# A hybrid mLSTM and attention layer: the first block's squares on two engines, its norm in two GpSimd operations, its rounded copy ahead of the weights' low parts

## The chip, the cores and the metric

The kernel runs on one core of a Trainium2 chip. The metric is the device time of one execution in microseconds (us). Before the change the median of three runs was 689.77 us (689.24 to 689.87).

The engines are called by their names or by the profile's short ones: TensorE (PE for matmuls, PEld for its weight loads), VectorE (DVE), ScalarE (ACT), GpSimd (POOL), SyncE (SP, which here only issues DMAs). Each engine has its own stream of instructions and works it off in order. Engines wait for each other by semaphores.

## The reference

The layer takes x (512 tokens by 1024 channels, float32). What the change touches is its start: the RMS norm of the rows and the first columns of one large projection.

```python
def rmsnorm(x, w):
    y = x * lax.rsqrt(jnp.mean(x * x, axis=-1, keepdims=True) + EPS)
    return y * w

h = rmsnorm(x, norm_w)
proj = jnp.einsum('bsd,de->bse', h, w_in) + b_in      # 1024 -> 11272 columns
# split of proj: mLSTM q, k, v, gates; attention q, k, v; output gates; merge gates
qs = rmsnorm(to_heads(sq, 8), sb_q_norm_w)
# ... mLSTM in chunks, stick-breaking attention, two projections, gated merge
out = x + jnp.einsum('bsd,de->bse', merged, w_out)
```

## The kernel before

All matmuls are made from float32 numbers split in a high part (rounded to the format that TensorE takes at full rate) and a low part (the rest). A product is three matmuls: high by high, low by high and high by low. For the activations the parts are called hh and hl, for the weights wh and wl, and for the weights of the first group fh and fl.

The work is a list of units in a fixed order, one slab of weights (512 KB) each. Each unit has a load (SP), a split (ScalarE writes the high part, VectorE the low part), 24 matmuls, and an evacuation from PSUM. Attention heads and mLSTM heads are interleaved with the units by a table of start numbers. Nothing in this order is decided at run time: every engine gets its instructions in the order in which the code emits them.

The first four units are special. They hold the weights of attention's q (512 columns of 1024 rows, in four slabs of 256 rows), and each of the four token blocks (tb, 128 tokens) passes through all of them, as soon as its own norm is done. For one block:

- `x_norm` (line 281): the sum of squares of each row. For block 0, whose x arrives in two halves, ScalarE squares one half after the other (line 289), and GpSimd adds the two sums (line 290). `rstd` (line 273) then turns the sum into r = (sum/1024 + eps)^-0.5 with two GpSimd operations.
- `x_mul` (line 296): VectorE multiplies x by r in place.
- `x_tp` (line 301): TensorE transposes x, eight times 128 by 128, into two PSUM tiles of four each.
- `x_hh` (line 307): VectorE reads one PSUM tile, multiplies by the norm's weights nw_t and writes hh, rounded. `x_hl` (line 313) writes hl = the same product minus hh, in four instructions per PSUM tile.
- `first_hi` (line 1158) writes the high parts fh of the weights on ScalarE, `first_lo` (line 1164) the low parts fl: for k = 2 and 3 on GpSimd, for the others on VectorE. k numbers the eight groups of 128 channels.
- `first_mm` (line 1208) emits the matmuls of one block: for block 0 those of k = 0 to 4, then the transposes of block 1, and then k = 5 to 7.

Ahead of all that, TensorE runs nine matmuls on zeros (`warm(9)`, line 1186). Then come `norm_vec` (line 229), which turns the norm's weights by a TensorE transpose and copies them to nw_t on VectorE, `x_scale(0)` (`x_norm` and `x_mul` of block 0) and two more matmuls on zeros. The order of the emission is:

```python
warm(9)
norm_vec()
x_scale(0)
warm(2)
first_hi(0); first_lo(0); first_lo(1)
x_turn(0)        # x_tp, x_hh, x_hl of each of the two PSUM tiles
first_hi(1); first_lo(2, nc.gpsimd); first_lo(3, nc.gpsimd)
x_norm(1); first_hi(2); first_lo(4); x_mul(1); first_lo(5)
```

Of the kernel before, what the change touches and what calls it, by code (L numbers as in the profile page):

```python
# [11 lines left out]
AF = mybir.ActivationFunctionType  # L12
OP = mybir.AluOpType

D = 1024
T = 512
KT = 8
TB = 4
NQK = 18
EPS = 1e-6  # L20
# [15 lines left out]
def tile_hybrid_layer(  # L36
# [16 lines left out]
    nc = tc.nc  # L53
# [21 lines left out]
    def blk(tag, dt=F32, shape=(512,), name=None, p=128):  # L75

        where = mp if tag in MISC else sp
        return where.tile([p] + list(shape), dt, name=name or tag, tag=tag, bufs=BUFS[tag])

    def two(tag, dt=F32, name=None):  # L80

        t = blk(tag, dt, (2, 512), name=name)
        return t[:, 0, :], t[:, 1, :]

    def dense_ps():
        return psd.tile([128, 512], F32, name="dps", tag="dps")

    def att_ps():
        return psa.tile([128, 512], F32, name="aps", tag="aps")
# [100 lines left out]
    def h_sta(k, tb):  # L190
        ts = slice(tb * 128, (tb + 1) * 128)
        return hh[:, k, ts], hl[:, k, ts]
# [27 lines left out]
    mhalf = cst.tile([128, 8], F32, name="mhalf")  # L220
# [6 lines left out]
    nw_t = cst.tile([128, 8], F32, name="nw_t")  # L227

    def norm_vec():
        vp = att_ps()  # L230
        nc.tensor.transpose(vp[:, 0:8], v_rows[0:8, :], ident[0:8, 0:8])
        nc.vector.tensor_copy(nw_t, vp[:, 0:8])

    def load_vecs():
        for j in range(4):
# [37 lines left out]
    def rstd(dst, ssq, n, eps):  # L273
        nc.gpsimd.tensor_scalar(dst, ssq, 1.0 / n, eps, op0=OP.mult, op1=OP.add)
        nc.gpsimd.tensor_tensor(dst, dst, mhalf[:, 0:dst.shape[1]], op=OP.pow)

    def x_scale(tb):
        x_norm(tb)
        x_mul(tb)

    def x_norm(tb):
        xs = tiny.tile([128, 4], F32, name="xs", bufs=2)
        ssq, r = xs[:, 0:2], xs[:, 2:3]
        xn = x_t[tb]
        junk = blk("om", BF, (D,), name="junk")
        if tb == 0:
            for i in range(2):
                c = slice(i * D // 2, (i + 1) * D // 2)
                nc.scalar.activation(junk[:, c], xn[:, c], AF.Square, accum_out=ssq[:, i:i + 1])
            nc.gpsimd.tensor_tensor(ssq[:, 0:1], ssq[:, 0:1], ssq[:, 1:2], op=OP.add)  # L290
        else:
            nc.scalar.activation(junk, xn, AF.Square, accum_out=ssq[:, 0:1])
        rstd(r, ssq[:, 0:1], D, EPS)
        x_r.append(r)

    def x_mul(tb):
# [4 lines left out]
    def x_tp(tb, g):  # L301
        tp = x_ps[tb, g] = att_ps()
        for j in range(4):
            kt = g * 4 + j
            nc.tensor.transpose(tp[:, j * 128:(j + 1) * 128], x_t[tb][:, kt * 128:(kt + 1) * 128], ident)  # L305

    def x_hh(tb, g):
        ks = slice(4 * g, 4 * g + 4)
        nc.vector.tensor_tensor(hh[:, ks, tb * 128:(tb + 1) * 128],
                                x_ps[tb, g].rearrange("p (k t) -> p k t", k=4),  # L310
                                nw_t[:, ks].unsqueeze(2).to_broadcast([128, 4, 128]), op=OP.mult)

    def x_hl(tb, *ks):
        ts = slice(tb * 128, (tb + 1) * 128)
        for k in ks:
            tp = x_ps[tb, k // 4][:, k % 4 * 128:k % 4 * 128 + 128]
            nc.vector.scalar_tensor_tensor(hl[:, k, ts], tp, nw_t[:, k:k + 1],  # L317
                                           hh[:, k, ts].bitcast(F32), op0=OP.mult, op1=OP.subtract)

    def x_turn(tb):  # L320
        for g in range(2):
            x_tp(tb, g)
            x_hh(tb, g)
            x_hl(tb, *range(4 * g, 4 * g + 4))
# [831 lines left out]
    f_w = []  # L1156

    def first_hi(i):
        his = two("qk", FR, name="fh")
        for j in range(2):  # L1160
            nc.scalar.activation(his[j], units[i].st[:, j, :], AF.Copy)
            f_w.append((his[j], blk("y", FR, name="fl")))

    def first_lo(k, engine=nc.vector):
        hi, lo = f_w[k]
        engine.tensor_tensor(lo, units[k // 2].st[:, k % 2, :], hi.bitcast(F32), op=OP.subtract)
# [15 lines left out]
    def warm(n):  # L1182
        for _ in range(n):
            nc.tensor.matmul(wp, idle[:, 0:128], idle, start=True, stop=True)

    warm(9)
    norm_vec()
    x_scale(0)
    warm(2)
    first_hi(0)  # L1190
    first_lo(0)
    first_lo(1)
    x_turn(0)
    first_hi(1)
    first_lo(2, nc.gpsimd)
    first_lo(3, nc.gpsimd)
    x_norm(1)
    first_hi(2)
    first_lo(4)
# [5 lines left out]

    f_ps = []

    def first_mm(tb):
        def mm(half):
            if half == 0:  # L1210
                f_ps.append(dense_ps())
            n = 4 if tb else 5
            for k in range(n) if half == 0 else range(n, KT):
                sh, sl = h_sta(k, tb)
                wh, wl = f_w[k]
                nc.tensor.matmul(f_ps[tb], sh, wh, start=k == 0, stop=False)  # L1216
                nc.tensor.matmul(f_ps[tb], sl, wh, start=False, stop=False)  # L1217
                nc.tensor.matmul(f_ps[tb], sh, wl, start=False, stop=k == KT - 1)  # L1218
        return mm

    for tb in range(TB):
        units[tb].mm = first_mm(tb)
# [40 lines left out]
    for c in range(N):  # L1263
# [15 lines left out]
        if c == 0:  # L1279
            x_tp(1, 0)  # L1280
            x_tp(1, 1)
            x_hh(1, 0)
            x_hl(1, 0, 1, 2, 3)
            x_norm(2)
            x_mul(2)
            x_hh(1, 1)
            x_hl(1, 4, 5, 6, 7)
            x_scale(3)
            gates_fill()
# [47 lines left out]
```

## Time and profile before

| | |
|---|---|
| median of the runs | 689.77 us |
| the profiled execution, its own time | 689.49 us |
| its span, first to last instruction | 687.8 us |
| TensorE matmuls busy | 681.0 us (99%) |
| VectorE | 467.2 us (68%) |
| ScalarE | 337.1 us (49%) |
| GpSimd | 111.7 us (16%) |

1.7 us of the execution's time lie outside the span. Times in rows count from the start of the span. A matmul's busy time is modelled and overlaps with the next one's, so the distance from one start to the next tells more than the duration. A row that merges several instructions has the time from the start of the first to the end of the last.

### The profile page before, as it was taken

The page shows a single profiled execution, that of the slowest core. Times are in us where ns is not written, and L with a number is a line of the kernel's source. Part 1 is how long each engine was busy: PE and PEld are TensorE (multiplying, and loading weights), DVE is VectorE, ACT ScalarE, POOL GpSimd, SP SyncE. Part 2 cuts the span into 40 slices and gives each one's busy share as a digit, 9 for nine tenths or more (in the row PEclk, how much of TensorE's full clock was granted, in tenths as well). Part 3 has the DMA queues.
Part 4 walks back from the last instruction along what each step waited for, and adds up shares of the span by engine and source line. Part 5 has one row for each costly group of instructions (what it writes and reads, how often), then busy time and mean ns, then how long its engine had stood idle before and what let it go on. Part 6 is the DMA issues. An engine that isn't in the chain of part 4 may idle for free.

```text
span 687.8 us, 9389 instructions
## 1 busy us (share of the span) xinstructions
PE 681.0 (99%) x3162; PEld 568.9 (83%) x3162; DVE 467.2 (68%) x819; ACT 337.1 (49%) x631; POOL 111.7 (16%) x266
## 2 busy tenths in 40 slices
PE   8999999999999999999999999999999999999997
PEld 5888888888888888888888888888888888888876
DVE  6746787777997886789834648994352364445997
ACT  6245465566455653344466533448554343344451
POOL 4122042365430310000001210000112000111020
PEclk9999999999999999999999999999999999999999
DMA  7433543435463533643341343434223456599333
GB/s 250 139 95 107 160 138 105 134 112 149 134 171 86 124 111 83 139 95 92 107 117 53 107 109 85 128 91 134 68 64 90 115 176 200 141 206 205 121 82 103
DMA packets 122289, 84.74 MB, mean 123 GB/s; under 512 B 19018, under 2 KB 105956, under 8 KB 122240
## 3 DMA queue, kind: packets, MB, share of 16 engines
q1 hardware_dynamic: 119600, 77.97, 40.3%
q0 software_dynamic: 2496, 6.03, 4.7%
q8 instruction: 25, 0.41, 0.2%
q14 instruction: 24, 0.20, 0.1%
q10 hardware_dynamic: 144, 0.13, 0.1%
HBM read 66.22 MB, written 2.15 MB: 99 GB/s over the span
## 4 chain that ended last, share of the span: by engine, by line
PE 98%; DVE 1%; DMA 1%; SPq 0%; issue 0%; ACT 0%
PE dps L92 28%; PE dps L93 27%; PE dps L94 27%; PE aps L93 3%; PE aps L94 3%; PE aps L92 3%; PE dps L1216 1%; PE dps L1217 1%; PE dps L1218 1%; PE aps L811 1%; PE aps L813 1%; PE aps L812 1%; DMA stg<-in_w_in_dram 1%; PE aps L305 0%; DVE hl L317 0%; PE aps L591 0%
## 5 line engine op out<-in xcount | busy, mean ns | idle before, releaser
L98 DVE TENSOR_TENSOR wl<-stg,wh 128x1024 fp32r<-128x1024 f32 x92 | 112.5, 1223 | 106.0 <-ACT wh L97 105.5
L92 PE MATMUL dps<-hh,wh 128*128 128x512 f32 x448 | 175.0, 391 | 0.0
L94 PE MATMUL dps<-hh,wl 128*128 128x512 f32 x448 | 174.4, 389 | 0.0
L93 PE MATMUL dps<-hl,wh 128*128 128x512 f32 x448 | 174.4, 389 | 0.0
L97 ACT ACTIVATE wh<-stg 128x1024 fp32r<-128x1024 f32 x92 | 96.8, 1052 | 64.5 <-PE dps L94 44.3
L94 PEld LDWEIGHTS dps<-hh,wl 128*128 128x128 f32 x448 | 84.1, 188 | 17.7
L93 PEld LDWEIGHTS dps<-hl,wh 128*128 128x128 f32 x448 | 84.2, 188 | 16.8
L92 PEld LDWEIGHTS dps<-hh,wh 128*128 128x128 f32 x448 | 84.1, 188 | 16.7
L92 PE MATMUL dps<-wh,hh 128*128 128x512 f32 x224 | 87.7, 392 | 0.0
L94 PE MATMUL dps<-wh,hl 128*128 128x512 f32 x224 | 87.3, 390 | 0.0
L93 PE MATMUL dps<-wl,hh 128*128 128x512 f32 x224 | 87.2, 389 | 0.0
L94 PEld LDWEIGHTS dps<-wh,hl 128*128 128x128 f32 x224 | 42.0, 188 | 9.0
L92 PEld LDWEIGHTS dps<-wh,hh 128*128 128x128 f32 x224 | 42.1, 188 | 8.3
L93 PEld LDWEIGHTS dps<-wl,hh 128*128 128x128 f32 x224 | 42.1, 188 | 8.2
L704 DVE SCALAR_TENSOR_TENSOR acc<-tmp,vec,acc 128x511 f32<-128x511 f32 (+2 forms) x48 | 36.0, 750 | 1.7
L707 ACT ACTIVATE tmp<-acc 128x512 f32<-128x512 f32 x16 | 10.1, 633 | 50.8 <-DVE acc L704 50.8
L480 POOL TENSOR_SCALAR_AFFINE_SELECT om<-om 128x128 f32<-128x128 f32 x32 | 15.3, 479 | 96.2 <-ACT om L478 96.1
L486 DVE TENSOR_TENSOR_SCAN om<-om 128x512 f32<-128x512 f32 (+3 forms) x32 | 26.7, 834 | 5.5 <-POOL om L480 5.5
L764 POOL TENSOR_SCALAR_AFFINE_SELECT w_all<-om 128x128 f32<-128x128 f32 x16 | 5.3, 363 | 144.4 <-DMA om<-rb_d 144.4
L478 ACT ACTIVATE om<-aps,rq 128x512 f32<-128x512 f32 (+3 forms) x32 | 16.8, 524 | 21.0 <-PE aps L94 21.0
L94 PE MATMUL dps<-yh,wl 128*128 128x512 f32 x64 | 24.9, 389 | 0.0
L92 PE MATMUL dps<-yh,wh 128*128 128x512 f32 x64 | 24.9, 389 | 0.0
(249 smaller groups left out, 1217.8 us busy)
## 6 DMA issues: line engine op xcount, KB each, us to landing
stg<-in_w_in_dram SPq DMA_DIRECT2D x87, 512.0 KB, 3.9
az<-ay SPq DMA_DIRECT2D x128, 40.0 KB, 2.9
stg<-in_w_proj_s_dram SPq DMA_DIRECT2D x8, 512.0 KB, 4.7
B<-in_w_out_dram SPq DMA_DIRECT2D x8, 512.0 KB, 6.6
stg<-in_w_proj_m_dram SPq DMA_DIRECT2D x8, 512.0 KB, 5.9
wl<-stg POOLq DMA_DIRECT2D x8, 512.0 KB, 5.9
tz<-ty SPq DMA_DIRECT2D x72, 32.0 KB, 1.9
brow<-in_b_in_dram SPq DMA_DIRECT2D x8, 256.0 KB, 4.5
```

The costliest lines, as they stand in the source:

```text
L92: nc.tensor.matmul(ps, ah, bh, start=first, stop=False)
L93: nc.tensor.matmul(ps, ah, bl, start=False, stop=False)
L94: nc.tensor.matmul(ps, al, bh, start=False, stop=last)
L97: nc.scalar.activation(hi, src, AF.Copy)
L98: nc.vector.tensor_tensor(lo, src, hi.bitcast(F32), op=OP.subtract)
L478: nc.scalar.activation(om[:, 0:n], zp, AF.Sigmoid, scale=rn[:, h:h + 1])
L480: nc.gpsimd.affine_select(out=om[:, ts], in_=om[:, ts], compare_op=OP.is_gt, fill=1.0, base=0, channel_multiplier=1, pattern=[[-1, 128]])
L486: nc.vector.tensor_tensor_scan(back, back, back, 1.0, op0=OP.mult, op1=OP.bypass)
L704: nc.vector.scalar_tensor_tensor(acc[:, j:], t[:, 0:T - j], cw(3 - j, ch), acc[:, j:], op0=OP.mult, op1=OP.add)
L707: nc.scalar.activation(t, acc, AF.Sigmoid)
L811: nc.tensor.matmul(nm[:, 0:258], ph, vh, start=j == 0, stop=False)
L812: nc.tensor.matmul(sum_v, ph, vl, start=False, stop=False)
```

## The change

Four things change, all in the first block's path.

1. The sum of squares of block 0: ScalarE squares only the first half; VectorE squares the second half, with a scalar_tensor_tensor that also accumulates.
2. The norm: GpSimd no longer adds the two sums in an operation of its own. One tensor_scalar adds both sums and 1024·eps, and the power follows. The factor 32 (the root of 1024) that this leaves out is put into nw_t, whose copy becomes a multiplication. The other blocks have the same form with two operations, as before.
3. On VectorE, hh of the first PSUM tile now stands ahead of fl of k = 0 and 1. On TensorE both transposed tiles are emitted first, as they were executed before.
4. TensorE's first six matmuls of block 0 are reordered: high by high of k = 0 and 1, then the two with fl, then the two with hl.

```diff
     def norm_vec():
         vp = att_ps()
         nc.tensor.transpose(vp[:, 0:8], v_rows[0:8, :], ident[0:8, 0:8])
-        nc.vector.tensor_copy(nw_t, vp[:, 0:8])
+        nc.vector.tensor_scalar(nw_t, vp[:, 0:8], 32.0, None, op0=OP.mult)
...
         if tb == 0:
-            for i in range(2):
-                c = slice(i * D // 2, (i + 1) * D // 2)
-                nc.scalar.activation(junk[:, c], xn[:, c], AF.Square, accum_out=ssq[:, i:i + 1])
-            nc.gpsimd.tensor_tensor(ssq[:, 0:1], ssq[:, 0:1], ssq[:, 1:2], op=OP.add)
+            a, b = xn[:, 0:D // 2], xn[:, D // 2:D]
+            nc.scalar.activation(junk[:, 0:D // 2], a, AF.Square, accum_out=ssq[:, 0:1])
+            nc.vector.scalar_tensor_tensor(junk[:, D // 2:D], b, 1.0, b, op0=OP.mult, op1=OP.mult,
+                                           accum_out=ssq[:, 1:2])
+            nc.gpsimd.tensor_scalar(r, ssq[:, 0:1], ssq[:, 1:2], D * EPS, op0=OP.add, op1=OP.add)
         else:
             nc.scalar.activation(junk, xn, AF.Square, accum_out=ssq[:, 0:1])
-        rstd(r, ssq[:, 0:1], D, EPS)
+            nc.gpsimd.tensor_scalar(r, ssq[:, 0:1], 1.0, D * EPS, op0=OP.mult, op1=OP.add)
+
+        nc.gpsimd.tensor_tensor(r, r, mhalf[:, 0:1], op=OP.pow)
         x_r.append(r)
...
     first_hi(0)
+    x_tp(0, 0)
+    x_tp(0, 1)
+    x_hh(0, 0)
     first_lo(0)
     first_lo(1)
-    x_turn(0)
+    x_hl(0, 0, 1, 2, 3)
+    x_hh(0, 1)
+    x_hl(0, 4, 5, 6, 7)
     first_hi(1)
...
+    def three(tb, k, *which):
+        sh, sl = h_sta(k, tb)
+        wh, wl = f_w[k]
+        for n in which:
+            nc.tensor.matmul(f_ps[tb], *((sh, wh), (sl, wh), (sh, wl))[n],
+                             start=(k, n) == (0, 0), stop=(k, n) == (KT - 1, 2))
...
             for k in range(n) if half == 0 else range(n, KT):
-                sh, sl = h_sta(k, tb)
-                wh, wl = f_w[k]
-                nc.tensor.matmul(f_ps[tb], sh, wh, start=k == 0, stop=False)
-                nc.tensor.matmul(f_ps[tb], sl, wh, start=False, stop=False)
-                nc.tensor.matmul(f_ps[tb], sh, wl, start=False, stop=k == KT - 1)
+
+                if tb or k > 1:
+                    three(tb, k, 0, 1, 2)
+                elif k == 0:
+                    three(tb, 0, 0)
+                    three(tb, 1, 0)
+                    three(tb, 0, 2)
+                    three(tb, 1, 2)
+                    three(tb, 0, 1)
+                    three(tb, 1, 1)
         return mm
```

The start of VectorE's stream before, with what each instruction waits for in brackets (a semaphore of an engine, or of a DMA queue, DMAHW; x is the block's x, xs the small tile with the sums and r):

```order
L1179 MEMSET idle 128x512
L232 COPY nw_t<-aps 128x8 [waits PE_49]
L297 TENSOR_SCALAR x<-x,xs 128x1024 [waits DMAHW0_49,DMAHW1_49,Activation_49,Pool_49]
L1166 TENSOR_TENSOR fl<-stg,fh 128x512 [waits DMAHW3_49,Activation_49]
L1166 TENSOR_TENSOR fl<-stg,fh 128x512 [waits Activation_49]
L309 TENSOR_TENSOR hh<-aps,nw_t 128x4x128 [waits DVE_49,PE_49]
L317 SCALAR_TENSOR_TENSOR hl<-aps,nw_t,hh 128x128 [waits DVE_49]
```

and the same place now:

```order
L1182 MEMSET idle 128x512
L232 TENSOR_SCALAR nw_t<-aps 128x8 [waits PE_49]
L289 SCALAR_TENSOR_TENSOR junk,xs<-x 128x512 [waits DMAHW1_49]
L300 TENSOR_SCALAR x<-x,xs 128x1024 [waits DVE_49,DMAHW0_49,Activation_49,Pool_49]
L312 TENSOR_TENSOR hh<-aps,nw_t 128x4x128 [waits PE_49]
L1169 TENSOR_TENSOR fl<-stg,fh 128x512 [waits DMAHW3_49,Activation_49]
L1169 TENSOR_TENSOR fl<-stg,fh 128x512 [waits Activation_49]
L320 SCALAR_TENSOR_TENSOR hl<-aps,nw_t,hh 128x128 [waits DVE_49]
```

The square (line 289) has come in between nw_t, which waits for TensorE, and the multiplication of x; hh stands ahead of the two fl.

TensorE's stream from the first group of zeros to the first matmuls of block 0, before:

```order
L1184 MATMUL dps<-idle 128x512 x9
L231 MATMUL aps<-ident,v_rows 128x8
L1184 MATMUL dps<-idle 128x512 x2
L305 MATMUL aps<-ident,x 128x128 x8
L1216 MATMUL dps<-fh,hh 128x512
L1217 MATMUL dps<-fh,hl 128x512
L1218 MATMUL dps<-fl,hh 128x512
L1216 MATMUL dps<-fh,hh 128x512
```

and now:

```order
L1187 MATMUL dps<-idle 128x512 x9
L231 MATMUL aps<-ident,v_rows 128x8
L1187 MATMUL dps<-idle 128x512 x2
L308 MATMUL aps<-ident,x 128x128 x8
L1220 MATMUL dps<-fh,hh 128x512 x2
L1220 MATMUL dps<-fl,hh 128x512 x2
L1220 MATMUL dps<-fh,hl 128x512 x2
L1220 MATMUL dps<-fh,hh 128x512
```

The transpose of the norm's weights (line 231) stays behind the nine matmuls on zeros; of the first six matmuls only the order is another.

## Rows read from the trace of the kernel before

**Rows 1.** What TensorE waited for, in the whole span: engine, line, who released it; us in total, times, longest.

```profile
PE dps L1184 <- DVE idle L1179: 1.5, 1, 1.5
PE dps L1216 <- DVE hh L309: 1.0, 1, 1.0
PE aps L305 <- DVE x L297: 0.8, 2, 0.6
```

**Rows 2.** Busy time in three stretches: from and to, length; then busy us (and instructions) of PE, PEld, DVE, ACT, POOL; clock, DMA share, GB/s.

```profile
9.20:13.20 4.00, 3.92 (x15) 2.69 (x15) 3.96 (x12) 3.49 (x7) 2.90 (x4) 1.00 1.06 405
...
14.20:653.00 638.80, 638.80 (x2975) 535.45 (x2974) 429.22 (x758) 313.97 (x597) 103.16 (x247) 1.00 0.45 121
...
657.50:684.00 26.50, 26.50 (x130) 22.39 (x128) 24.68 (x36) 9.39 (x12) 1.77 (x2) 1.00 0.33 90
```

**Rows 3.** Two pieces of the chain that ended last, in order of time: start, us, what.

```profile
6.48 0.64 ACT fh L1161
...
12.47 0.76 DVE x L297
```

**Rows 4.** VectorE's timeline of the first 18 us: start, us, instruction, count, idle time before it and its releaser.

```profile
5.81 0.17 DVE L232 COPY nw_t<-aps 128x8 f32<-128x8 f32 x1 [4.36 <-PE aps L231]
6.26 0.75 DVE L297 TENSOR_SCALAR x<-x,xs 128x1024 f32<-128x1024 f32 x1 [0.28 <-POOL xs L275]
7.14 1.29 DVE L1166 TENSOR_TENSOR fl<-stg,fh 128x512 fp32r<-128x512 f32 x2
8.35 0.68 DVE L309 TENSOR_TENSOR hh<-aps,nw_t 128x512 fp32r<-128x512 f32 x1
9.07 1.13 DVE L317 SCALAR_TENSOR_TENSOR hl<-aps,nw_t,hh 128x128 fp32r<-128x128 f32 x4
...
12.47 0.74 DVE L297 TENSOR_SCALAR x<-x,xs 128x1024 f32<-128x1024 f32 x1
13.14 0.68 DVE L1166 TENSOR_TENSOR fl<-stg,fh 128x512 fp32r<-128x512 f32 x1
13.74 1.28 DVE L1166 TENSOR_TENSOR fl<-P,fh 128x512 fp32r<-128x512 f32 x2
...
16.70 1.37 DVE L297 TENSOR_SCALAR x<-x,xs 128x1024 f32<-128x1024 f32 x1
```

**Rows 5.** ScalarE's timeline at the start, the same columns.

```profile
3.55 0.63 ACT L289 ACTIVATE junk<-x 128x512 bf16<-128x512 f32 x1 [1.49 <-DMA x<-in_x_dram]
...
4.30 0.63 ACT L289 ACTIVATE junk<-x 128x512 bf16<-128x512 f32 x1
4.84 0.19 ACT L289 ACTIVATION_READ_ACCUMULATOR junk<-x 128x1 f32 x1
```

**Rows 6.** GpSimd's timeline of the first 18 us.

```profile
5.11 0.19 POOL L290 TENSOR_TENSOR xs<-xs 128x1 f32<-128x1 f32 x1 [3.67 <-ACT junk L289]
5.39 0.19 POOL L274 TENSOR_SCALAR xs<-xs 128x1 f32<-128x1 f32 x1
5.66 0.56 POOL L275 TENSOR_TENSOR xs<-xs,mhalf 128x1 f32<-128x1 f32 x1
8.79 2.56 POOL L1166 TENSOR_TENSOR fl<-stg,fh 128x512 fp32r<-128x512 f32 x2 [2.57 <-ACT fh L1161]
11.43 0.19 POOL L274 TENSOR_SCALAR xs<-xs 128x1 f32<-128x1 f32 x1
...
14.46 0.62 POOL L274 TENSOR_SCALAR xs<-xs 128x1 f32<-128x1 f32 x1 [2.19 <-ACT junk L292]
...
16.56 0.96 POOL L572 MEMSET wg<- 128x1024 f32 x1
```

**Rows 7.** TensorE's timeline up to the first matmul of block 0.

```profile
1.50 4.11 PE L1184 MATMUL dps<-idle 128*128 128x512 f32 x9 [1.50 <-DVE idle L1179]
5.55 0.22 PE L231 MATMUL aps<-ident,v_rows 8*128 8x8 f32 x1
5.70 0.73 PE L1184 MATMUL dps<-idle 128*128 128x512 f32 x2
7.07 1.09 PE L305 MATMUL aps<-ident,x 128*128 128x128 f32 x8 [0.63 <-DVE x L297]
9.18 0.47 PE L1216 MATMUL dps<-fh,hh 128*128 128x512 f32 x1 [1.02 <-DVE hh L309]
```

**Rows 8.** Groups of instructions on VectorE by line, operation and shape: count, busy us, mean ns of one, idle us before them and its releaser.

```profile
L710 DVE SCALAR_TENSOR_TENSOR tmp<-acc,tmp 128x512 f32<-128x512 f32 x16 | 11.0, 688 | 2.7 <-ACT tmp L707 2.7
L486 DVE TENSOR_TENSOR_SCAN om<-om 128x512 f32<-128x512 f32 x8 | 9.8, 1227 | 5.1 <-POOL om L480 5.1
...
L487 DVE TENSOR_TENSOR a_all<-a_all,om 128x256 f32<-128x256 f32 x8 | 3.6, 452 | 0.8
```

**Rows 9.** GpSimd's timeline at 94.3 us, one row.

```profile
94.26 0.29 POOL L483 TENSOR_SCALAR_AFFINE_SELECT a_all<-a_all 128x128 f32<-128x128 f32 x1
```

**Rows 10.** VectorE's timeline at the same moment.

```profile
94.32 0.51 DVE L487 TENSOR_TENSOR a_all<-a_all,om 128x256 f32<-128x256 f32 x1
```

**Rows 11.** GpSimd's timeline at 137 us.

```profile
137.14 0.82 POOL L378 TENSOR_SCALAR rq<-rq 128x4 f32<-128x4 f32 x1
```

**Rows 12.** VectorE's timeline at the same moment.

```profile
136.64 1.22 DVE L98 TENSOR_TENSOR wl<-stg,wh 128x1024 fp32r<-128x1024 f32 x1 [2.67 <-ACT wh L97]
137.78 0.68 DVE L98 TENSOR_TENSOR qtt<-tz,qtt 128x512 fp32r<-128x512 f32 x1
```

## The prediction

> **What bounds the kernel now.** First the list of what TensorE waited for. It has three entries in the whole span: 1.5 us for the zeros, 1.0 us for the first hh and 0.8 us for the scaled x, all in the first 14 us [rows 1]. Next the busy time by stretches: from 14.20 us on TensorE is busy for every microsecond, 638.80 of 638.80 and 26.50 of 26.50 [rows 2]. So whatever moves the end of the start-up moves the end of the kernel by as much, and no later wait takes it up. Third the chain of waits: it runs through ScalarE's fh at 6.48 us and then through VectorE up to the multiplication of block 1's x at 12.47 us, to which TensorE's transposes of block 1 are tied [rows 3]. That multiplication is the gate. TensorE can do the matmuls of block 0 early or late, but behind k = 4 it needs block 1's x. Last the timelines of the engines, for how VectorE gets from 7.14 us, where its dense work begins, to that gate at 12.47 us: 5.33 us without a pause of note [rows 4].
>
> **What the change moves, step by step.**
>
> *The square on VectorE.* Before, ScalarE squared the halves at 3.55 and 4.30 us, the second accumulator was read by 5.03 us [rows 5], and GpSimd added (5.11), scaled (5.39) and took the power (5.66 to 6.22) [rows 6]. VectorE multiplied x at 6.26 us [rows 4]. Now VectorE's half of the square is emitted behind nw_t, and nw_t waits for TensorE's transpose of the norm's weights, which stands behind the nine matmuls on zeros and ran at 5.55 to 5.77 us [rows 7]. nw_t ran at 5.81 to 5.98 us after 4.36 us of idling [rows 4]. VectorE works in order, so the square can't start before about 5.95 us, although its half of x was there by 4.30 us, when ScalarE began on it without a wait [rows 5]. Queued behind it are x's multiplication and all that follows; GpSimd's sum waits for it, and TensorE for both.
>
> The trace has no such square. Its nearest rows are the scalar_tensor_tensor of the same size, 0.69 us, and as an upper end the scan of that size, 1.23 us [rows 8]. I take 0.69, the same operation, and 0.10 for reading the accumulator, which on ScalarE ended that much behind the ACTIVATE (4.93 against 5.03 [rows 5]). Below zero it can't be. The sum is there at 5.95 + 0.69 + 0.10 = 6.74 us.
>
> *The norm in two operations.* GpSimd starts 0.08 us later (as 5.03 to 5.11), the power 0.27 us after that (5.39 to 5.66) and takes 0.56 us, and VectorE follows 0.04 us behind [rows 4, 6]: 6.82, 7.09, 7.65, and x's multiplication at 7.69 us. That is 1.43 us later than before. The removed addition is worth 0.28 us (5.11 to 5.39 [rows 6]) and is contained in this. The factor 32 in nw_t costs nothing: one instruction on 8 columns for another; half or double its 0.17 us would move the sum by no more than 0.2.
>
> *hh ahead of fl.* x's multiplication takes 0.75 us, to 8.44. TensorE begins 0.06 us later (7.01 to 7.07 [rows 4, 7]) at 8.50. Eight transposes took 1.09 us, so the first four are out after about 0.62, and hh starts near 9.16 us. Before, the two fl filled just this wait (7.14 to 8.35 [rows 4]); now VectorE idles there and does them afterwards. Its sum up to the gate stays nearly as it was: hl behind hh cost 0.72 us from start to start because it needs hh, and an unrelated instruction 0.60 (13.14 to 13.74) [rows 4], so 5.33 becomes 5.21. Without any collision the gate would be at 9.16 + 5.21 = 14.37 us, 1.90 later. The matmuls' new order gains nothing, because TensorE waits at the gate anyway.
>
> *The collision.* Before, VectorE's two fl were over at 8.43 us, and GpSimd's two fl ran from 8.79 to 11.35 us beside hh and hl, which read PSUM [rows 4, 6]. GpSimd's start hangs on ScalarE and the weights and stays. VectorE's fl now come at 9.76 us, in the middle of them, and all four read two operands from SBUF. The trace shows that such pairs don't run side by side. VectorE's multiplication at 16.70 us took 1.37 us instead of 0.74 while a GpSimd memset ran from 16.56 [rows 4, 6]. GpSimd's 0.19 us operation took 0.62 at 14.46 us, when VectorE was in an fl [rows 4, 6]. A VectorE tensor_tensor that began 0.06 us into a GpSimd select took 0.51 us, with a mean of 0.452 for its form [rows 8 to 10], as if it had started 0.17 us before the select's end. And a GpSimd operation that came in during a VectorE subtraction ended 0.10 us behind it, although the next VectorE subtraction was already queued [rows 11, 12]: whoever waits gets in between two instructions.
>
> So I have them take turns. GpSimd's first fl holds until 8.79 + 1.28 - 0.17 = 9.90; VectorE's first goes from 9.90 to 10.58; GpSimd's second, due at 10.07, gets in at about 10.50 and holds until 10.50 + 1.28 - 0.17 = 11.61; VectorE's second starts there, and hl 0.60 later at 12.21 us, against 9.07 before [rows 4]. That is 3.14 us, and from hl to the gate nothing differs. The second block's r is ready well before the gate: GpSimd's two operations on it follow on its second fl with 0.83 us between them (5.39 to 6.22 [rows 6]).
>
> The Trainium skill, "SBUF — State Buffer", section "Who interferes with whom", states the rule in the same sense: a VectorE instruction with two SBUF inputs and a GpSimd instruction that reads SBUF exclude each other for the whole instruction, and who issues first decides. The rows agree except that the hold ended some 0.17 us before the end of GpSimd's row; by the whole instruction it would be 0.3 us more.
>
> **The sum.** All else being dense, 3.14 us goes to the end: 689.49 us for the profiled execution + 3.14 = 692.63. The median of the runs was 0.28 us above that execution, so I say 692.7. With the long square (1.23), hh moves to 9.70 and both GpSimd fl go ahead of VectorE's: hl at about 12.45, 692.9.
>
> **Rivals.**
>
> *No turns.* VectorE keeps its place for both fl once it has it (9.90, 10.50, hl at 11.10: +2.03, 691.5), or doesn't collide at all (+1.90, 691.4). For it: two VectorE instructions overlap by 0.08 us at their seam (two fl in 1.29 us [rows 4]). Against it: rows 11 and 12.
>
> *The clock falls.* The nine first matmuls started 0.45 us apart (5.55 - 1.50 over nine [rows 7]), which fits the 1.2 GHz level; dense ones later 0.215 (638.80 over 2975 [rows 2]), 2.4 GHz. TensorE now idles from 6.43 to 8.50 us and does little until 12.4. If that brings the lower level back, and it lasts as long as in the beginning, nine matmuls behind the gate cost 0.235 us more each: +2.1, 694.7. Against it: idling for 0.63 and 1.02 us left the level up (fifteen instructions in 4.00 us with waits [rows 2, 7]). For it: the idling is twice as long.
> "TensorE: Matmul & The Clock Gate" in the Trainium skill, section "What's actually happening", says that the low level is the default and that activity lifts it; no row here shows it falling.
>
> *Side by side after all, not slower.* If the transpose of the norm's weights comes early enough, the square really runs beside ScalarE's. Its place is nw_t: it has to be done by 4.30 us instead of 5.98, which nine matmuls at the higher level would do (1.50 + 9 x 0.215 = 3.4). Then the sum is there at 5.09, x's multiplication starts at 6.04, hh at 7.51, and the two fl run from 8.11, mostly ahead of GpSimd's; hl at 9.31 is still 0.24 later than before: 689.7, no difference. Against it: the zeros ran at the low level here, and TensorE does nothing before them that could change that. The change then does what its words say, and gains nothing, since VectorE's sum to the gate is the same.
>
> **How the numbers follow.** Taking turns has 0.54, no turns 0.26, the clock on top of either 0.12, side by side 0.06, and 0.02 is for a gain that I don't see. The range 690.9 to 694.4 takes in the first two and their unknown terms and leaves out most of the third and all of the fourth, under 0.2. What a measurement of this kernel can tell from no change is about 0.2%, 1.38 us. Both likely cases lie beyond it; slower is 0.89, within it 0.08, faster 0.03.
>
> **What would show it.** In the profile of the changed kernel: nw_t still near 5.8 us and the square right behind it; x's multiplication near 7.7 us instead of 6.26; hh near 9.2; VectorE's fl longer than 0.68 us or spread out, and GpSimd's second fl delayed to end near 11.8; the gate at about 15.6 us. TensorE must wait for several microseconds more in the first 16 us and nowhere else. A square that starts before 5 us, or a gate at 12.5, would prove me wrong; a gate near 14.4 would say that the collision is not there.

## The result and the profile after

The kernel after takes 693.40 us (median of six runs, 692.51 to 694.09), the kernel before on the same chip 689.85 (689.24 to 690.50): 1.0050 times as long, interval 1.0037 to 1.0063. The prediction said 692.7, range 690.9 to 694.4, slower. The profiled execution after took 692.51 us, 3.02 more than the one before (689.49); its span is 690.8 us.

First the list of what TensorE waited for, over the whole span (total us, times, longest):

```profile
PE aps L308 <- DVE x L300: 2.3, 2, 2.1
PE dps L1187 <- DVE idle L1182: 1.5, 1, 1.5
PE dps L1220 <- DVE fl L1169: 0.5, 1, 0.5
```

Against [rows 1] the wait for the scaled x has grown from 0.8 to 2.3 us, the wait for hh has gone from the list, and one for fl has come. That is only 1.0 us more waiting (4.3 us against 3.3). The other two microseconds are busy time, which rose from 681.0 to 682.9 us. Where, the busy time by stretches shows, with the columns of [rows 2]:

```profile
9.20:13.20 4.00, 3.95 (x13) 2.35 (x12) 3.61 (x8) 3.55 (x7) 3.32 (x4) 0.62 1.04 412
13.20:17.20 4.00, 3.30 (x19) 2.30 (x17) 3.96 (x10) 1.78 (x3) 0.74 (x2) 1.00 0.23 32
...
24.00:653.00 629.00, 629.00 (x2927) 527.25 (x2927) 418.95 (x738) 309.21 (x586) 100.58 (x242) 1.00 0.45 120
```

The granted clock is 0.62 on the mean from 9.20 to 13.20 us, where it was 1.00 before: TensorE is "busy" there at a lower clock, most of the time at half speed. From 24 us on it is busy for every one of 629.00 us, as before. All of the difference lies in the start-up.

VectorE's timeline (start, us, instruction, count, idle time before it and its releaser):

```profile
5.84 0.17 DVE L232 TENSOR_SCALAR nw_t<-aps 128x8 f32<-128x8 f32 x1 [4.39 <-PE aps L231]
5.92 0.68 DVE L289 SCALAR_TENSOR_TENSOR junk<-x 128x512 bf16<-128x512 f32 x1
6.53 0.08 DVE L289 DVE_READ_ACCUMULATOR junk<-x 128x1 f32 x1
7.80 0.75 DVE L300 TENSOR_SCALAR x<-x,xs 128x1024 f32<-128x1024 f32 x1 [1.19 <-POOL xs L296]
9.59 0.69 DVE L312 TENSOR_TENSOR hh<-aps,nw_t 128x512 fp32r<-128x512 f32 x1 [1.03 <-PE aps L308]
10.19 2.00 DVE L1169 TENSOR_TENSOR fl<-stg,fh 128x512 fp32r<-128x512 f32 x2
12.11 1.11 DVE L320 SCALAR_TENSOR_TENSOR hl<-aps,nw_t,hh 128x128 fp32r<-128x128 f32 x4
...
15.50 0.74 DVE L300 TENSOR_SCALAR x<-x,xs 128x1024 f32<-128x1024 f32 x1
```

Three things answer to [rows 4]. The square stands right behind nw_t, and x's multiplication at 7.80 instead of 6.26. The two fl, back to back, took 2.00 us instead of 1.29. The last row is the gate, block 1's x: 15.50 instead of 12.47, 3.03 us later, which is the 3.02 us of the whole execution. GpSimd's timeline at the same time:

```profile
6.81 0.31 POOL L291 TENSOR_SCALAR xs<-xs 128x1 f32<-128x1 f32 x1 [5.37 <-DVE junk L289]
7.20 0.57 POOL L296 TENSOR_TENSOR xs<-xs,mhalf 128x1 f32<-128x1 f32 x1
8.53 2.51 POOL L1169 TENSOR_TENSOR fl<-stg,fh 128x512 fp32r<-128x512 f32 x2 [0.76 <-ACT fh L1164]
```

GpSimd's two fl ran undisturbed, 2.51 us as before (2.56 in [rows 6]), to 11.04 us. They began 0.26 us earlier than in [rows 6], at 8.53 instead of 8.79, released by ScalarE's fh. VectorE's began behind them: 10.19 + 2.00 - 1.29 = 10.90, so its first was held until about 0.14 us before the end of GpSimd's row. And TensorE:

```profile
8.62 1.79 PE L308 MATMUL aps<-ident,x 128*128 128x128 f32 x8 [2.15 <-DVE x L300]
10.43 1.19 PE L1220 MATMUL dps<-fh,hh 128*128 128x512 f32 x2
11.64 1.10 PE L1220 MATMUL dps<-fl,hh 128*128 128x512 f32 x2
...
15.64 0.50 PE L1220 MATMUL dps<-fl,hh 128*128 128x512 f32 x1 [0.54 <-DVE fl L1169]
16.30 1.09 PE L308 MATMUL aps<-ident,x 128*128 128x128 f32 x8 [0.16 <-DVE x L300]
```

After 2.15 us without work the eight transposes took 1.79 us, where they took 1.09 in [rows 7]. The chain of waits (start, us, what) has the first four of them, on which hh hangs:

```profile
8.62 0.95 PE aps L308 x4
```

### The profile page after: what moved, and what is told of

Read it like the earlier page. It is cut to its first block, busy times and chain, and to the rows that moved or that the text cites. A ratio compares the mean times of both kernels' runs of the same rounds, so it can differ in the third digit from the quotient of the medians.

```text
span 690.8 us, 9388 instructions
## 1 busy us (share of the span) xinstructions
PE 682.9 (99%) x3162; PEld 569.6 (82%) x3162; DVE 467.8 (68%) x821; ACT 336.3 (49%) x629; POOL 112.5 (16%) x265
## 3 DMA queue, kind: packets, MB, share of 16 engines
HBM read 66.22 MB, written 2.15 MB: 99 GB/s over the span
## 4 chain that ended last, share of the span: by engine, by line
PE 98%; DVE 1%; issue 0%; POOL 0%; DVEq 0%; POOLq 0%
PE dps L92 27%; PE dps L94 27%; PE dps L93 27%; PE aps L93 3%; PE aps L94 3%; PE aps L92 3%; PE dps L1220 3%; PE aps L814 1%; PE aps L816 1%; PE aps L815 1%; PE dps L1187 1%; PE aps L308 1%; DVE fl L1169 0%; PE aps L594 0%; PE aps L593 0%; PE aps L458 0%
## 5 line engine op out<-in xcount | busy, mean ns | idle before, releaser
L93 PE MATMUL dps<-yl,wh 128*128 128x512 f32 x64 | 24.9, 389 | 0.0
```

The lines of the kernel that those rows point to most:

```text
L93: nc.tensor.matmul(ps, ah, bl, start=False, stop=False)
```

## The experiments

Theory: the change costs because the square stands behind nw_t, and because VectorE's fl now meet GpSimd's fl. Rivals: the clock alone costs the time; the new order of hh and the matmuls costs it, wherever the square is; the norm in two operations costs it. Each kernel was timed in five rounds beside the kernel before, whose median was 689.78 us beside the first four and 689.98 beside the last four.

One relation makes the profiles easy to compare. The transposes of block 1 started at 13.28 us in the profile before and at 16.30 after; taken from the executions' own times, 689.49 and 692.51, both leave 676.21 us. So an execution's time should be that start plus 676.2, unless something new happens later.

### The square ahead of nw_t

```diff
     warm(9)
+    x_norm(0)
     norm_vec()
-    x_scale(0)
+    x_mul(0)
```

> The changed kernel with one edit: VectorE's square is emitted ahead of nw_t, so that it need not wait for TensorE's transpose of the norm's weights. If the square's place behind nw_t is the cause, VectorE squares before 5 us, x's multiplication starts near 6.1 instead of 7.80 us and hh near 7.5 instead of 9.59. VectorE's first fl then goes ahead of GpSimd's. If the two engines take turns, VectorE's second fl waits for GpSimd's first, hl starts near 10.4, the gate (block 1's multiplication of x) is near 13.8 and the time near 690.8. If they don't take turns: hl 9.3, gate 12.7, 689.7. If the square's place isn't the cause, the time stays at 693 (692.5 to 694.1).

Measured 690.98 us (689.86 to 694.26, 11 runs), ratio 1.0009 (0.9994 to 1.0023). VectorE's timeline:

```profile
4.19 0.69 DVE L289 SCALAR_TENSOR_TENSOR junk<-x 128x512 bf16<-128x512 f32 x1 [2.74 <-DMA x<-in_x_dram]
...
8.20 2.37 DVE L1169 TENSOR_TENSOR fl<-stg,fh 128x512 fp32r<-128x512 f32 x2
10.49 1.11 DVE L320 SCALAR_TENSOR_TENSOR hl<-aps,nw_t,hh 128x128 fp32r<-128x128 f32 x4
...
13.88 0.75 DVE L300 TENSOR_SCALAR x<-x,xs 128x1024 f32<-128x1024 f32 x1
```

and GpSimd's:

```profile
8.33 3.39 POOL L1169 TENSOR_TENSOR fl<-stg,fh 128x512 fp32r<-128x512 f32 x2 [2.27 <-ACT fh L1164]
```

The square now waits only for its half of x and starts at 4.19 us. The gate comes back from 15.50 to 13.88 and the median by 2.4 us; the interval now takes in no difference from the kernel before. Most of what is left at the gate (1.41 us against [rows 4]) is the collision: VectorE was first by 0.13 us (8.20 against 8.33), then GpSimd got in between VectorE's two. The pair took 2.37 us, 1.08 more than in [rows 4], and GpSimd's 3.39 instead of 2.51.

### The old order, with the square behind nw_t

```diff
     first_hi(0)
-    x_tp(0, 0)
-    x_tp(0, 1)
-    x_hh(0, 0)
     first_lo(0)
     first_lo(1)
-    x_hl(0, 0, 1, 2, 3)
-    x_hh(0, 1)
-    x_hl(0, 4, 5, 6, 7)
+    x_turn(0)
```

The six matmuls also went back to their old order.

> The changed kernel with parts 3 and 4 undone: fl of k = 0 and 1 stand ahead of hh again, and the matmuls are in the old order; the square stays behind nw_t. x's multiplication stays near 7.8 us. Turns: VectorE's first fl at 8.5, GpSimd's first gets in at 9.1, VectorE's second waits for it to 10.2, hl 11.5, gate 14.9, 691.9. No turns: fl at 8.5 and 9.1, hl 10.4, gate 13.8, 690.8. If the new order is what costs the 3 us by itself, the time is back at 689.9.

Measured 693.63 us (691.29 to 695.09, 6 runs), ratio 1.0050 (1.0034 to 1.0066): as slow as the kernel after. VectorE did what was expected (its fl pair again 2.37 us, the gate at 14.99), but TensorE did not. Its timeline, and the busy time of one stretch with the granted clock third from the end:

```profile
11.71 0.77 PE L1215 MATMUL dps<-fh,hh 128*128 128x512 f32 x1 [1.44 <-ACT fh L1164]
...
15.26 0.63 PE L1215 MATMUL dps<-fl,hh 128*128 128x512 f32 x1
...
17.25 1.03 PE L308 MATMUL aps<-ident,x 128*128 128x128 f32 x8
```

```profile
12.00:14.00 2.00, 2.00 (x6) 1.62 (x6) 1.96 (x7) 1.85 (x3) 0.80 (x3) 0.50 0.96 294
```

The row puts the wait of 1.44 us down to ScalarE's fh, but hh, which ran from 10.88 to 11.56 us, ended 0.15 us ahead of the first matmul, just as it did before [rows 4, 7]; the wait was for hh. After waits of 2.15 and 1.44 us TensorE ran at half the clock until some time before 16 us, its matmuls about 0.43 us apart. The transposes of block 1 show no wait; they stand behind matmuls that were late themselves, at 17.25 instead of about 15.8 (the gate, 0.75 us of multiplication, 0.06). The clock cost 1.5 us here, and the forecast missed it. 17.25 + 676.2 = 693.45 agrees with this execution (693.37). So in the old order the square's place alone, with the collision that it brings, makes the kernel as slow as the whole change does: 2.5 us through VectorE (14.99 against 12.47) and 1.5 through the clock.

### fl behind the first hl

```diff
     x_hh(0, 0)
+    x_hl(0, 0, 1, 2, 3)
     first_lo(0)
     first_lo(1)
-    x_hl(0, 0, 1, 2, 3)
     x_hh(0, 1)
```

On TensorE the two matmuls with hl went ahead of the two with fl.

> The changed kernel with VectorE's two fl behind the first four hl (and TensorE's fl matmuls behind its hl matmuls), so that they run after GpSimd's two fl (which end near 11.0) and collide with nothing. By the collision theory the pair takes 1.29 instead of 2.00 us, the gate moves from 15.5 to 14.8 and the time falls by 0.7 us against the changed kernel, to 691.8 (like its profiled run) or 692.7 (like its median). If the longer pair has another cause, it takes 2.00 us again and the time stays.

Measured 692.22 us (691.80 to 693.25, 5 runs), ratio 1.0036 (1.0024 to 1.0048). VectorE's timeline:

```profile
11.20 1.28 DVE L1169 TENSOR_TENSOR fl<-stg,fh 128x512 fp32r<-128x512 f32 x2
...
14.76 0.75 DVE L300 TENSOR_SCALAR x<-x,xs 128x1024 f32<-128x1024 f32 x1
```

GpSimd's two fl ran from 8.79 to 11.30 us here, so VectorE's came at their very end: 1.28 us for the pair, as in [rows 4], instead of 2.00. The gate moved to 14.76, 0.74 earlier than after. 0.16 of this is hh, at 9.43 instead of 9.59, because the transposes still ran at a granted clock of 1.00 here (1.10 us for the eight). From hh to the gate VectorE took 5.33 us instead of 5.91, and that part is the collision taken out. The median is 1.2 us lower than after, though the two intervals overlap. The four hl that took the place beside GpSimd's fl read one operand from PSUM, and lost nothing by it (1.12 us, 1.13 in [rows 4]).

### More work for TensorE's clock

```diff
-    warm(2)
+    warm(11)
```

> The changed kernel with eleven instead of two matmuls on zeros in TensorE's wait for x, to about 8.3 us. If the clock's fall (transposes 1.79 instead of 1.09 us, granted clock 0.62 from 9.2 to 13.2 us) comes from that wait, the clock stays at 1.00 and hh starts near 9.3 instead of 9.59. In the profiled run GpSimd's second fl held VectorE's first to 10.9 anyway, so the gate hardly moves: 692.5. If the low clock is also why the changed kernel's median lies 0.9 us above its profiled run, the median falls from 693.4 to 692.5 as well and the runs draw together. If the clock has no part in it, the median stays at 693.4.

Measured 692.74 us (692.61 to 692.87, 5 runs), ratio 1.0040 (1.0028 to 1.0052). Busy time by stretches and VectorE's timeline:

```profile
10.00:12.00 2.00, 1.16 (x6) 0.51 (x4) 2.00 (x3) 1.76 (x5) 1.92 (x4) 1.00 1.06 426
```

```profile
10.53 1.88 DVE L1169 TENSOR_TENSOR fl<-stg,fh 128x512 fp32r<-128x512 f32 x2
...
15.72 0.75 DVE L300 TENSOR_SCALAR x<-x,xs 128x1024 f32<-128x1024 f32 x1
```

With zeros in its idle time TensorE kept the clock at 1.00 throughout; they ended late and pushed the transposes to 9.28 us, so hh came at 9.92 instead of 9.59 and the gate at 15.72 instead of 15.50. All the same the median is 692.74 instead of 693.40, and the runs lie within 0.26 us of each other instead of 1.58. That points to the clock for a part of the kernel after's scatter; it doesn't show it, since the two intervals overlap and the next kernel, which keeps the clock up too, has the old median. The clock alone doesn't make the slowness: with the clock up, 2.96 us against the kernel before are left.

### Fewer zeros

```diff
-    warm(2)
+    warm(7)
```

> The changed kernel with seven instead of two matmuls on zeros in TensorE's wait for x, so that they end near 7.7 to 8.4 us, before x is there at 8.6, and delay nothing. The clock's fall needs TensorE's long wait: by that theory the granted clock is 1.00 from 9 to 17 us, transposes take 1.09 us, hh starts near 9.3, the gate stays at 15.5 because GpSimd's second fl is ahead of VectorE's, and the time is 692.5 in all runs. If the clock has no part in the median, it is 693.4 with the same spread as the changed kernel (1.6 us).

Measured 693.37 us (693.02 to 693.98, 5 runs), ratio 1.0047 (1.0034 to 1.0060): a miss. The clock stayed at 1.00 and hh came at 8.91 us, 0.68 earlier than after. Only 0.28 of that is the clock's; for the rest nw_t ran at 5.44 us instead of 5.84, since the nine zeros ahead of it, which the edit doesn't touch, were over sooner in this execution. But then, VectorE:

```profile
5.44 0.17 DVE L232 TENSOR_SCALAR nw_t<-aps 128x8 f32<-128x8 f32 x1 [3.99 <-PE aps L231]
...
9.52 3.04 DVE L1169 TENSOR_TENSOR fl<-stg,fh 128x512 fp32r<-128x512 f32 x2
12.48 1.11 DVE L320 SCALAR_TENSOR_TENSOR hl<-aps,nw_t,hh 128x128 fp32r<-128x128 f32 x4
...
15.87 0.74 DVE L300 TENSOR_SCALAR x<-x,xs 128x1024 f32<-128x1024 f32 x1
```

ScalarE and GpSimd:

```profile
8.34 1.15 ACT L1164 ACTIVATE fh<-stg 128x512 fp32r<-128x512 f32 x2 [0.51 <-DMA stg<-in_w_in_dram]
...
9.05 2.96 POOL L1169 TENSOR_TENSOR fl<-stg,fh 128x512 fp32r<-128x512 f32 x2 [1.68 <-ACT fh L1164]
```

and TensorE, which waits for each of the two fl:

```profile
10.93 0.49 PE L1220 MATMUL dps<-fl,hh 128*128 128x512 f32 x1 [0.48 <-DVE fl L1169]
12.61 0.50 PE L1220 MATMUL dps<-fl,hh 128*128 128x512 f32 x1 [1.19 <-DVE fl L1169]
```

Here the turns of the prediction appear one by one: GpSimd's first, VectorE's first (done shortly before 10.93), GpSimd's second, VectorE's second (done shortly before 12.61). The pair costs 3.04 us, and hl comes no earlier than after (12.48 against 12.11). A part of that is another accident: ScalarE had the second slab of weights late (8.34 us, after 7.82), so GpSimd's fl began at 9.05 instead of 8.53. Counted from GpSimd's start, hl came 3.43 us later here and 3.58 after. In this execution 0.8 us came on top late in the kernel, where TensorE waited for weights from a DMA. All five runs had a mean clock of 0.998 to 1.000, and still the median is that of the kernel after: by the forecast's own terms that speaks against the clock as what holds the median up.

### The norm alone, and the order alone

The kernel before with only part 2 of the change:

```diff
-        nc.vector.tensor_copy(nw_t, vp[:, 0:8])
+        nc.vector.tensor_scalar(nw_t, vp[:, 0:8], 32.0, None, op0=OP.mult)
...
-            nc.gpsimd.tensor_tensor(ssq[:, 0:1], ssq[:, 0:1], ssq[:, 1:2], op=OP.add)
+            nc.gpsimd.tensor_scalar(r, ssq[:, 0:1], ssq[:, 1:2], D * EPS, op0=OP.add, op1=OP.add)
...
-        rstd(r, ssq[:, 0:1], D, EPS)
+            nc.gpsimd.tensor_scalar(r, ssq[:, 0:1], 1.0, D * EPS, op0=OP.mult, op1=OP.add)
+        nc.gpsimd.tensor_tensor(r, r, mhalf[:, 0:1], op=OP.pow)
```

> The kernel before with part 2 alone: the norm in two GpSimd operations, 32 in nw_t; both squares stay on ScalarE and all orders stay. r is there some 0.15 to 0.28 us earlier, but VectorE's fl then wait for the weights' high parts at 7.1 us as before, so the gate stays at 12.5 and the time at 689.8. If VectorE's chain to the gate hangs on r instead, the time falls by up to 0.28 us; if the operation with two scalars costs, it rises.

Measured 689.96 us (689.23 to 693.31, 12 runs), ratio 1.0008 (0.9998 to 1.0019): no difference clear of the noise. Its profiled execution was the slowest of the twelve and tells something else. TensorE's waits and one row of ScalarE's timeline:

```profile
PE dps L1217 <- DVE hh L310: 3.0, 1, 3.0
```

```profile
8.31 1.15 ACT L1162 ACTIVATE fh<-stg 128x512 fp32r<-128x512 f32 x2 [3.42 <-DMA stg<-in_w_in_dram]
```

The first slab of weights landed late: ScalarE began fh at 8.31 us, in the profile before at 6.48 [rows 3]. VectorE's fl waited for that, hh behind them, and TensorE for hh, 3.0 us. Then the clock was 0.50 from 10 to 16 us, and block 1's transposes came at 17.18 us without the change's square at all.

The kernel before with only parts 3 and 4:

```diff
     first_hi(0)
+    x_tp(0, 0)
+    x_tp(0, 1)
+    x_hh(0, 0)
     first_lo(0)
     first_lo(1)
-    x_turn(0)
+    x_hl(0, 0, 1, 2, 3)
+    x_hh(0, 1)
+    x_hl(0, 4, 5, 6, 7)
```

On TensorE the six matmuls of block 0 took the new order.

> The kernel before with parts 3 and 4 alone: hh of the first four k ahead of fl, and the matmuls' new order; squares and norm as before. x's multiplication at 6.26, hh at 7.75, VectorE's first fl at 8.35, ahead of GpSimd's at 8.5 to 8.8. By turns GpSimd's first gets in at 8.95, VectorE's second at 10.1, hl at 10.7, 1.6 us later than before, gate 14.1, 691.4. Without turns: hl 9.5, 690.3. If the new order were a gain by itself: under 689.8.

Measured 690.47 us (690.29 to 691.57, 11 runs), ratio 1.0010 (1.0001 to 1.0018). The profiled execution, 691.57, was again the slowest; in it VectorE and GpSimd met:

```profile
8.85 2.37 DVE L1166 TENSOR_TENSOR fl<-stg,fh 128x512 fp32r<-128x512 f32 x2
...
14.53 0.75 DVE L297 TENSOR_SCALAR x<-x,xs 128x1024 f32<-128x1024 f32 x1
```

The new order costs about 0.5 us at the median, barely clear of the noise, and gains nothing. The gate's 2.06 us in this execution aren't the order's alone: ScalarE's second square waited 0.61 us for its half of x, and x's multiplication ran at 6.74 us instead of 6.26. Whether the fl met in the other runs too can't be seen, as only one is profiled.

### The square ahead of nw_t, in the old order

The first experiment's edit together with the second's: the square ahead of nw_t, the norm in two operations, the rest as before.

> The square on VectorE ahead of nw_t, the norm in two operations, and the old order of hh, fl and the matmuls. x's multiplication near 6.1, fl at 7.1 as soon as the weights' high parts are there, over by 8.4 and so ahead of GpSimd's; hh at 8.3, hl at 9.1, gate 12.5: 689.8, as before. So a side-by-side square that starts in time gains nothing and costs nothing. If VectorE's extra square costs by itself, the time is above 690.5; if the earlier r helps, below 689.5.

Measured 690.28 us (689.31 to 692.93, 11 runs), ratio 1.0003 (0.9991 to 1.0014). VectorE's timeline:

```profile
4.28 0.69 DVE L289 SCALAR_TENSOR_TENSOR junk<-x 128x512 bf16<-128x512 f32 x1 [2.83 <-DMA x<-in_x_dram]
...
7.14 1.29 DVE L1169 TENSOR_TENSOR fl<-stg,fh 128x512 fp32r<-128x512 f32 x2 [0.21 <-ACT fh L1164]
...
9.07 1.13 DVE L320 SCALAR_TENSOR_TENSOR hl<-aps,nw_t,hh 128x128 fp32r<-128x128 f32 x4
...
12.47 0.74 DVE L300 TENSOR_SCALAR x<-x,xs 128x1024 f32<-128x1024 f32 x1
```

and ScalarE's:

```profile
3.43 0.63 ACT L288 ACTIVATE junk<-x 128x512 bf16<-128x512 f32 x1 [1.36 <-DMA x<-in_x_dram]
```

From fl at 7.14 to the gate at 12.47 these are the starts of [rows 4]. The square now starts as soon as its half of x is there, and it gains nothing, for two reasons. It isn't side by side with ScalarE's even so: that one ran from 3.43 to 4.06 us, and VectorE's waited for its half of x until 4.28 (in the square-first kernel 3.40 to 4.03, and 4.19). VectorE's accumulator was read by 4.97, where ScalarE alone had read both by 5.03 [rows 5]. And behind x's multiplication VectorE waits for ScalarE's fh, which hangs on the weights. No version that was run is faster than the kernel before beyond the noise.

## Why the prediction was right

Seen from the profiled execution, the prediction was right to 0.12 us (692.63 expected, 692.51 measured) and the gate to 0.11 (15.61 and 15.50). The parts under it fit less well, and two errors nearly cancel: GpSimd's fl began 0.26 us earlier than assumed (8.53 for 8.79), and from there to hl it took 0.16 us more (3.58 for 3.42). That the match is so close is luck. GpSimd's start hangs on the landing of the weights and lay between 8.33 and 9.11 us in nine of the ten profiles (10.36 in the one with a late first slab); where VectorE has to wait for GpSimd, the gate moves with it.

- **The square behind nw_t: right, and the main cause.** nw_t at 5.84 (5.81 expected to stay), the square at 5.92, its accumulator read out by 6.61 (6.74 expected; the read took 0.08 us). With the square ahead of nw_t, 1.20 of the median's 3.55 us were left; with the old order as well 0.30, within the noise.
- **The norm: a term mis-sized.** GpSimd's sum with two scalar operands took 0.31 us, not the 0.19 of the operations it replaces, and began 0.20 us behind the accumulator, not 0.08. x's multiplication came at 7.80 instead of 7.69. Of the 0.28 us that the removed addition was to be worth, 0.04 was left: from the accumulator to x's multiplication it took 1.19 us, and 1.23 before.
- **hh: late by 0.43 us against the prediction** (9.59 for 9.16). 0.11 is the norm, the rest the transposes at the lower clock: 0.95 us for the first four in the chain of waits, 0.62 expected.
- **The collision: mechanism right, sequence another in the profiled execution.** With hh that late, and GpSimd that early, GpSimd's two fl both went first, and VectorE's pair waited once: from its first fl to hl 1.92 us, where turns would have taken 2.45 (9.76 to 12.21). hl came at 12.11 for 12.21. The sign that I had named, GpSimd's second fl pushed back to end near 11.8 us, did not show: it ended at 11.04. The turns as written are those of the experiment with seven zeros, where hl came 3.43 us behind GpSimd's start (3.42 by the prediction). One of the rows cited for the rule was of another kind: the multiplication at 16.70 us reads one large operand, and the memset beside it reads none. What two fl do to each other is shown by the runs here.
- **From hl to the gate: right**, 3.39 us (12.11 to 15.50) and 3.40 before.
- **The rival "the clock falls": given 0.12, and it happened.** In the profiled execution it cost TensorE's time but little at the gate, because TensorE caught up before 15.5 us. So the sign that TensorE would wait for several microseconds more failed as well: it waited 1.0 us more, and the rest is work at the lower clock. My argument against it, that idling leaves the level up, rested on waits of 0.63 and 1.02 us, and didn't hold for 2.15. That the first nine matmuls ran at the low level I had from their spacing alone (0.45 us; 0.43 in the old-order kernel at a granted 0.50): the granted clock of the profile reads 1.00 there.
- **The median: the step from the profiled execution to the median failed in size.** I added 0.28 us as before; it was 0.89. The cause stays open. For the clock: three of the five other runs had a mean clock of 0.995, the value of the execution in which the clock cost 1.5 us, and with eleven zeros the median was 0.66 us lower. Against it: two runs with mean clocks of 0.999 and 1.000 took 693.38 and 694.09 us, and with seven zeros, where the clock stayed up, the median was 693.37. Turns as with seven zeros, or a late slab of weights, could hold such runs up; that isn't shown, because only one run of a kernel is profiled.

The experiments add up. All times in us; the gate and the transposes are those of the profiled execution, and the last column is its time less the transposes' start:

| kernel | first fl: VectorE / GpSimd | VectorE's fl pair | gate | block 1's transposes | profiled | rest |
|---|---|---|---|---|---|---|
| before | 7.14 / 8.79 | 1.29 | 12.47 | 13.28 | 689.49 | 676.21 |
| after | 10.19 / 8.53 | 2.00 | 15.50 | 16.30 | 692.51 | 676.21 |
| square first | 8.20 / 8.33 | 2.37 | 13.88 | 14.69 | 690.90 | 676.21 |
| old order | 8.59 / 8.73 | 2.37 | 14.99 | 17.25 | 693.37 | 676.12 |
| fl behind hl | 11.20 / 8.79 | 1.28 | 14.76 | 15.61 | 691.80 | 676.19 |
| eleven zeros | 10.53 / 8.73 | 1.88 | 15.72 | 16.52 | 692.74 | 676.22 |
| norm only | 8.98 / 10.36 | 1.29 | 14.31 | 17.18 | 693.31 | 676.13 |
| order only | 8.85 / 9.11 | 2.37 | 14.53 | 15.34 | 691.57 | 676.23 |
| square first, old order | 7.14 / 8.87 | 1.29 | 12.47 | 13.27 | 691.07 | 677.80 |
| seven zeros | 9.52 / 9.05 | 3.04 | 15.87 | 16.67 | 693.98 | 677.31 |

The rest is one number within 0.1 us, but for the last two rows, in which TensorE waited 1.1 and 0.8 us for weights late in the kernel (0.5 and 0.3 more stay unexplained). Apart from those waits the start-up decides.

## What to carry to other kernels

An engine works in order: before an operation is given to an idle engine, look at what its stream waits for at that place. VectorE had idled for 4.36 us, but behind an instruction that waited for TensorE, and the square was free only one place ahead of it. Ask as well when the second engine's share of the data arrives: here the second half of x landed when ScalarE was already done with squaring the first, so there was nothing to divide. When an instruction is moved, look also at which instruction of the other engine it now runs beside, and keep VectorE's reads of two SBUF operands away from GpSimd's. And where a later gate on the same engine sets the end, as VectorE's sum up to block 1's x here, an earlier start of another chain gains nothing.

## What was unexpected

**Being first counts, and hardly how early the second comes.** What VectorE's fl pair costs hangs on the moment at which it meets GpSimd's, as the table shows: 2.37 us when VectorE was first by 0.13 to 0.26 us (one GpSimd fl gets in between), 3.04 when it was second by 0.47 (both get in), 2.00 and 1.88 when it was second by 1.66 and 1.80 (it waits for what is left), and 1.28 at the end. These times contain the wait. Counted from GpSimd's start, VectorE's pair was over after 2.11 to 2.24 us in the first case, and after 3.51, 3.66 and 3.68 in the next three: as the second, coming 1.19 us earlier gained 0.15. Other work put into the gap made the wait free, with fl behind the first hl. The Trainium skill, "SBUF — State Buffer", section "Who interferes with whom", says that whoever issues first holds the shared ports for the whole instruction. The trace agrees, instruction by instruction, except that VectorE got in some 0.14 us before the end of GpSimd's row.

**The clock falls in a start-up.** Busy time by stretches in the kernel after, with the granted clock third from the end:

```profile
8.00:10.00 2.00, 1.39 (x8) 1.39 (x8) 0.97 (x2) 1.91 (x3) 1.47 (x2) 0.71 1.03 401
10.00:12.00 2.00, 1.95 (x5) 0.78 (x3) 2.00 (x3) 1.77 (x5) 1.92 (x3) 0.50 1.05 421
```

From 6 to 8 us it was still 1.00. It fell to 0.50 (1.2 GHz of 2.4) when the eight transposes had begun, behind 2.15 us without work: 0.85 on the mean from 8.5 to 9.0 us, 0.50 from 9.0. It stayed at 1.00 through 1.18 us of waiting in the square-first kernel and through idling of 1.00 us with seven zeros. "TensorE: Matmul & The Clock Gate" in the Trainium skill, section "What's actually happening", calls the low level the default, from which activity releases the array; this trace agrees in so far as it shows the low level coming back in the middle of a kernel, and the clock at 1.00 again from 14 us on, behind a run of matmuls.

**The runs can scatter upward for a cause outside the change.** A first slab of weights that landed late (fh at 8.31 us instead of 6.48) cost the norm-only kernel 3.8 us by the same two steps, a wait at VectorE and the lower clock behind it: 693.31 us against 689.49 for the profiled execution before. A single run of such a kernel says little about a change of one microsecond.
